# Hybrid decoder layer: last slots of four experts gathered and transposed as one tile, and 8 KB runs in the expert weight loads

## Chip, cores and metric

One core of one Trainium2 chip. The metric is the device time of one execution, in microseconds (us). The kernel before took 2277.39 us (median of 3 runs, 2274.5 to 2284.35).

## What is computed

A decoder layer on 2048 tokens of width 1024, all in float32. A mixer (gated linear attention and dilated attention) comes first; the change is in what follows it:

```
h = h + W_out [A ; B]
n = RMSNorm(h)
group  = argmax of 4 group logits;  two of its 8 experts by top-2   (32 experts in all)
h = h + sum over the two: gate * ( silu(n @ w1[e]) * (n @ w3[e]) ) @ w2[e]
y = RMSNorm(h)
```

w1 and w3 of an expert are 1024 x 512, w2 is 512 x 1024.

## The kernel before

The program is written in Tile: the code gives the data flow, and a scheduler that simulates the engines' time fixes the order of each engine's instructions when the program is built. On the chip every engine works through its list in order.

**Middle stage** (`mid`, lines 806 to 965, some 1183 to 1345 us). For each of 16 tiles of 128 tokens: output projection, residual, norm, router. VectorE writes the normed tile n2 in two halves of 512 columns (line 879); it is stored to HBM (line 880), and TensorE transposes it in blocks of 128 columns (line 891) against router weights loaded with row k*128 + p on partition p (lines 823, 824). `route` counts, for each expert, the slots that its tokens take, and scatters (token, gate) entries into a table in HBM. Each expert has 160 fixed slots: the first 128 are a full tile G, the last 32 a small tile R. Tokens beyond 160 would be done in a loop at the end, which does not run here.

**Expert stage** (`moe`, from line 1138). The loop at line 1371 runs over the 32 experts. In iteration e:
- `weights(e)` issues six loads of 1 MB on SyncE's queue (SP, line 1247): two halves each of w1, w3 and w2, into six buffers `raw`. A partition gets four rows of 2 KB that lie 128 rows apart (w1, w3), or two of 4 KB (w2). ScalarE (ACT) rounds each to `hi`, and VectorE (DVE) forms `lo` = raw - hi (line 1252).
- `gather(e + 2)` fetches, by indirect DMA on GpSimd (POOL), the 128 tokens of G (line 1263) and the 32 of R (line 1266).
- `up` multiplies the full tile in 48 matmuls (lines 1297 to 1299: hi by nh, hi by nl, lo by nh), and the 32 last slots by the unsplit weights in 32 matmuls (line 1306, two records each), four at a time in column groups: the remainder matmuls. They are the last readers of `raw`. Then h = silu * product (lines 1309, 1310; for the last slots 1314, 1315).
- `across` transposes h (line 1321) and the last slots' hr (line 1329) for the second product; ACT and DVE copy the results to hh, hl (line 1324) and ht (line 1331).
- `turn` transposes G of expert e + 1, eight blocks of 128 x 128 (line 1273), into tp, the only buffer of its pool in PSUM (2 of the 8 banks); ACT makes nh and DVE nl from it (line 1276). Then it transposes R, eight blocks of 32 x 128 (line 1281), and DVE copies it to nr (line 1283).
- `down` makes the second product: 24 matmuls for the full tile (lines 1343 to 1345), 16 remainder matmuls (line 1358, from ht), and adds both to HBM by indirect DMA (lines 1350, 1362).

For experts 0 and 1, G and a common R of 64 rows are gathered before the loop (lines 954 to 962). `entries` (line 1156) loads the table into SBUF: `it` for the full tiles, and `ir` four times, on each quarter of the partitions, for the last slots; these loads stand on SP's queue ahead of expert 1's weights.

Of the kernel before, what the change touches and what calls it, by code (L numbers as in the profile page):

```python
# [8 lines left out]
F32 = mybir.dt.float32  # L9
# [15 lines left out]
NE = 32  # L25
# [31 lines left out]
class Layer:  # L57
# [748 lines left out]
    def mid(self, st):  # L806
# [15 lines left out]
        nc.gpsimd.memset(rw, 0.0)  # L822
        nc.sync.dma_start(rw[:, :, 0:4], a["router_group_w"][0].rearrange("(k p) c -> p k c", p=128))
        nc.sync.dma_start(rw[:, :, 4:36], a["router_expert_w"][0].rearrange("(k p) c -> p k c", p=128))
        rb = keep.tile([128, NR], F32, name="rb")
# [32 lines left out]
        def project(i, between, oh, ol, h):  # L858
            rows = slice(i * 128, (i + 1) * 128)
            ss = wk.tile([128, 2], F32, name="ss")  # L860
            n2 = wk.tile([128, D], F32, name="n2")
            for f in range(2):
                pp = mm.tile([128, 512], F32, name="mm")
                fs = slice(f * 512, (f + 1) * 512)
                for k in range(4):
                    nc.tensor.matmul(pp, oh[:, k, :], woh[:, k, fs], start=k == 0, stop=False)
                    nc.tensor.matmul(pp, oh[:, k, :], wol[:, k, fs], start=False, stop=False)
                    nc.tensor.matmul(pp, ol[:, k, :], woh[:, k, fs], start=False, stop=k == 3)
                nc.vector.tensor_tensor(h[:, fs], pp, h[:, fs], OP.add)
                nc.scalar.activation(n2[:, fs], h[:, fs], AF.Square, accum_out=ss[:, f:f + 1])  # L870
                if f == 0:
                    between()
                    nc.vector.tensor_scalar(ss[:, 0:1], ss[:, 0:1], 1.0 / D, EPS, OP.mult, OP.add)
            nc.sync.dma_start(self.acc[rows, :], h)
            nc.vector.scalar_tensor_tensor(ss[:, 1:2], ss[:, 1:2], 1.0 / D, ss[:, 0:1], op0=OP.mult, op1=OP.add)
            nc.gpsimd.tensor_tensor(ss[:, 1:2], ss[:, 1:2], self.mhalf, OP.pow)
            for f in range(2):
                fs = slice(f * 512, (f + 1) * 512)
                nc.vector.scalar_tensor_tensor(n2[:, fs], h[:, fs], ss[:, 1:2], g2[:, fs], op0=OP.mult, op1=OP.mult)
            nc.sync.dma_start(self.n2[rows, :], n2)  # L880
            return n2
# [73 lines left out]
        R = self.e_in.tile([64, D], F32, name="R")  # L955
        self.first = {e: (G[e], R[32 * e:32 * e + 32], 32 * e) for e in range(2)}
        idx = rt.tile([128, 3], I32, name="idx", bufs=1)
# [180 lines left out]
    def moe(self):  # L1138
        tc, nc, a = self.tc, self.nc, self.a
        with self.moest as st:  # L1140
# [13 lines left out]
            i4A = keep.tile([128, NE], I32, name="i4")  # L1154

            def entries(es):

                ld = [nc.sync.dma_start(itA[:, es], table[0:128, es])]
                for g in range(4):
                    ld.append(nc.sync.dma_start(irA[32 * g:32 * g + 32, es], table[128:160, es]))  # L1160
                for l in ld:
                    for st in self.entries:
                        tc.add_manual_dep(l.ins, st.ins.name, mybir.DependencyInfo(mybir.DependencyClass.Sync, mybir.DependencyReason.DATA),
                                          reason="the whole table is read")
                f4 = gp.tile([128, NE], F32, name="f4", bufs=1)
                nc.vector.tensor_copy(f4[:, es], irA[:, es, 0])
                nc.vector.tensor_scalar(f4[:, es], f4[:, es], 4.0, self.gcol, OP.mult, OP.add)
                nc.vector.tensor_copy(i4A[:, es], f4[:, es])
# [66 lines left out]
            def weights(e, after={}):  # L1235

                parts = []
                for name, kk, n in (("expert_w1", 8, 512), ("expert_w3", 8, 512), ("expert_w2", 4, 1024)):
                    w = a[name][0, e] if isinstance(e, int) else a[name][0, bass.ds(e, 1)].rearrange("o k n -> (o k) n")
                    w = w.rearrange("(k p) n -> p k n", p=128)  # L1240
                    for half in range(2):
                        ks = slice(half * kk // 2, (half + 1) * kk // 2)
                        parts.append((w[:, ks, :], kk // 2, n))
                out = []
# [15 lines left out]
            def gather(e):  # L1260
# [3 lines left out]
                                             in_offset=bass.IndirectOffsetOnAxis(ap=itA[:, e, 0:1], axis=0))  # L1264
                R = gp.tile([32, D], F32, name="R")
                nc.gpsimd.indirect_dma_start(out=R, out_offset=None, in_=self.n2,
                                             in_offset=bass.IndirectOffsetOnAxis(ap=irA[0:32, e, 0:1], axis=0))
                return G, R

            def turn(G, R, at=0):  # L1270
                tp = tps.tile([128, KD, 128], F32, name="tp")
# [4 lines left out]
                self.turned = nc.scalar.copy(nh, tp), nc.vector.tensor_tensor(nl, tp, nh.bitcast(F32), OP.subtract)  # L1276
                if R is None:
                    return nh, nl, None
                tr = rps.tile([128, KD, 32], F32, name="r")
                for k in range(KD):  # L1280
                    nc.tensor.transpose(tr[:, k, :], R[:, k * 128:(k + 1) * 128], self.ident[at:at + 32, at:at + 32])
                nr = gp.tile([128, KD, 32], F32, name="nr")
                nc.vector.tensor_copy(nr, tr)  # L1283
                return nh, nl, nr

            def up(w, x):
                nh, nl, nr = x
                ps = []
# [19 lines left out]
                h = gp.tile([128, 512], F32, name="h")  # L1308
                nc.scalar.activation(h, ps[0], AF.Silu)
                nc.vector.tensor_tensor(h, ps[1], h, OP.mult)  # L1310
                hr = None
                if nr is not None:
                    hr = gp.tile([128, 256], F32, name="hr")
                    nc.scalar.activation(hr[64:128], pr[0:64], AF.Silu)
                    nc.vector.tensor_tensor(hr[64:128], pr[64:128], hr[64:128], OP.mult)
                return h, hr
# [47 lines left out]

            G = self.first
            x = turn(*G.pop(0))
            entries(slice(0, NE))
# [3 lines left out]
            for e in range(NE):  # L1371
                w1, w3, w2 = weights(e, held.get(e, lambda: {})())
                if e + 2 < NE:
                    G[e + 2] = gather(e + 2)
                h = across(*up((w1, w3), x))
                if e + 1 < NE:
                    x = turn(*G.pop(e + 1))
                    for t, c in zip(self.turned, self.crossed):
                        self.behind(t, c, "what the tensor engine waits for comes first")
# [13 lines left out]
            with tc.For_i(0, n, 1) as i:  # L1393
# [9 lines left out]
                w1, w3, w2 = weights(e)  # L1403
                x = turn(gx, None)
                down(w2, across(*up((w1, w3), x)), it, None)
# [96 lines left out]
```

## Time and profile before

| | |
|---|---|
| median of 3 runs | 2277.39 us |
| the profiled execution | 2277.6 us, of which the span is 2275.7 us |
| busy, share of the span | TensorE (PE) 92%, VectorE 56%, ScalarE 46%, GpSimd 22% |
| DMA | 440.32 MB, mean 193 GB/s over the span |
| loads of expert weights | 192, 1024 KB each, median 15.0 us from issue to landing |

The span runs from the first to the last instruction of the profiled execution. Idle time of an engine is put down to whatever released it last. A busy PE is not PE at its peak: matmuls overlap, so the time that one costs is read from the starts of successive ones. PEld is the weight load of TensorE, SP the queue that issues most transfers.

### The profile page before, as it was taken

The numbers are of one execution on the slowest core, as the hardware profiler recorded it, in microseconds if no ns is written. First come the engines' busy times: TensorE is split into PE (matmuls) and PEld (weight loads), VectorE is DVE, ScalarE is ACT, GpSimd is POOL, SyncE is SP. The second block draws the span as 40 slices with busy tenths as digits, with TensorE's granted clock in tenths as the row PEclk, the third lists the DMA queues.
The fourth block names the chain that finished last, engine by engine and source line by source line (L and its number), as shares of the span: only waits on it lengthen the run. The fifth ranks groups of instructions, "written<-read, shape, count | busy, mean of one in ns | idle before, by whom it ended". The sixth has DMA issues, their size and how long they took to land. (4 is left out here: it accounts for less than half of the span.)

```text
span 2275.7 us, 38854 instructions
## 1 busy us (share of the span) xinstructions
PE 2100.7 (92%) x15426; PEld 1566.0 (69%) x15426; DVE 1270.2 (56%) x2481; ACT 1056.1 (46%) x1805; POOL 509.6 (22%) x370
## 2 busy tenths in 40 slices
PE   7999999999996999999949967899999999999990
PEld 7799889799885665656637645566776677666660
DVE  5203436524336556666646564666777777677763
ACT  5413335523323466666714333555555555555552
POOL 2000000000002014152300241642233322233245
PEclk9999999999998999999979978999999999999995
DMA  8333333333318335444368737789988998888976
GB/s 257 116 113 93 108 128 103 124 100 111 107 66 275 103 98 142 126 136 98 85 167 296 250 80 215 230 291 298 306 288 277 301 299 303 291 275 293 302 254 233
DMA packets 248106, 440.32 MB, mean 193 GB/s; under 512 B 34497, under 2 KB 106594, under 8 KB 246626
## 3 DMA queue, kind: packets, MB, share of 16 engines
q1 hardware_dynamic: 198130, 351.39, 46.0%
q0 software_dynamic: 21840, 60.36, 10.5%
q10 hardware_dynamic: 27952, 26.05, 3.9%
q8 instruction: 123, 2.02, 0.4%
q14 instruction: 61, 0.50, 0.1%
HBM read 345.88 MB, written 92.40 MB: 193 GB/s over the span
## 5 line engine op out<-in xcount | busy, mean ns | idle before, releaser
L1252 DVE TENSOR_TENSOR lo<-raw,hi 128x2048 fp32r<-128x2048 f32 x192 | 439.2, 2290 | 163.7 <-ACT hi L1252 162.4
L1252 ACT CAST hi<-raw 128x2048 fp32r<-128x2048 f32 x192 | 365.6, 1906 | 253.7 <-DMA raw<-expert_w 218.8
L565 ACT ACTIVATE P<-P,st 128x256 f32<-128x256 f32 (+1 forms) x384 | 173.9, 455 | 112.7 <-DVE st L563 110.6
L214 PE MATMUL mm<-whi,nh 128*128 128x256 f32 x768 | 219.8, 286 | 0.0
L216 PE MATMUL mm<-whi,nl 128*128 128x256 f32 x768 | 218.0, 284 | 0.0
L215 PE MATMUL mm<-wlo,nh 128*128 128x256 f32 x768 | 217.6, 283 | 0.0
L1299 PE MATMUL mm<-lo,nh 128*128 128x512 f32 x512 | 203.7, 398 | 1.1 <-DVE lo L1252 1.1
L1297 PE MATMUL mm<-hi,nh 128*128 128x512 f32 x512 | 203.1, 397 | 1.0 <-ACT hi L1252 0.9
L1298 PE MATMUL mm<-hi,nl 128*128 128x512 f32 x512 | 200.4, 391 | 0.0
L129 POOL TENSOR_TENSOR ss<-ss,mhalf 128x1 f32<-128x1 f32 (+3 forms) x40 | 34.5, 864 | 696.3 <-DVE ss L128 694.8
L1350 POOL DMA_INDIRECT acc<-y,it x32 | 91.8, 2868 | 370.0 <-ACT y L1347 368.6
L563 DVE CUSTOM_DVE_ANT_0 P<-s,amask 128x256 f32<-128x256 f32 (+1 forms) x384 | 124.9, 362 | 75.3 <-PE s L559 58.8
L191 PE MATMUL mm<-nh,whi 128*128 128x512 f32 x384 | 154.5, 402 | 0.0
L1306 PE MATMUL r<-raw,nr 128*32 128x256 f32 x2048 | 152.7, 388 | 1.0 <-DVE nr L1283 0.5
L192 PE MATMUL mm<-nl,whi 128*128 128x512 f32 x384 | 153.1, 399 | 0.0
L193 PE MATMUL mm<-nh,wlo 128*128 128x512 f32 x384 | 152.7, 398 | 0.0
L214 PEld LDWEIGHTS mm<-whi,nh 128*128 128x128 f32 x768 | 145.2, 189 | 2.1 <-issue 0.7
L215 PEld LDWEIGHTS mm<-wlo,nh 128*128 128x128 f32 x768 | 145.5, 189 | 0.8 <-DVE wlo L177 0.4
L216 PEld LDWEIGHTS mm<-whi,nl 128*128 128x128 f32 x768 | 144.8, 189 | 0.1
L559 PE MATMUL s<-k,q 64*128 64x256 f32 (+1 forms) x768 | 137.5, 416 | 0.0
L1362 POOL DMA_INDIRECT acc<-yr,i x32 | 93.5, 2923 | 159.8 <-DMA acc<-y,it 148.8
L177 DVE TENSOR_TENSOR wlo<-raw,whi 128x1024 fp32r<-128x1024 f32 x48 | 57.0, 1221 | 112.7 <-ACT whi L176 112.7
(326 smaller groups left out, 4228.7 us busy)
## 6 DMA issues: line engine op xcount, KB each, us to landing
raw<-expert_w SPq DMA_DIRECT2D x192, 1024.0 KB, 15.0
raw<-w_in ACTq DMA_DIRECT2D x48, 512.0 KB, 4.9
fb<-fac SPq DMA_DIRECT2D x32, 384.0 KB, 7.6
x<-x SPq DMA_DIRECT2D x16, 512.0 KB, 5.2
og<-og SPq DMA_DIRECT2D x32, 256.0 KB, 3.3
xr<-x SPq DMA_DIRECT2D x32, 256.0 KB, 2.9
v<-av SPq DMA_DIRECT2D x8, 1024.0 KB, 6.1
hp<-xr SPq DMA_DIRECT2D x32, 256.0 KB, 2.5
```

The lines of the kernel that those rows point to most:

```text
L191: nc.tensor.matmul(ps, hi[:, k, ms], nh[q][:, k, :], start=k == 0, stop=False)
L192: nc.tensor.matmul(ps, hi[:, k, ms], nl[q][:, k, :], start=False, stop=False)
L193: nc.tensor.matmul(ps, lo[:, k, ms], nh[q][:, k, :], start=False, stop=k == KD - 1)
L214: nc.tensor.matmul(ps[:, j, :], h, hi[:, k, :], start=j == 0 and k == 0, stop=False, skip_group_check=True)
L215: nc.tensor.matmul(ps[:, j, :], h, lo[:, k, :], start=False, stop=False, skip_group_check=True)
L216: nc.tensor.matmul(ps[:, j, :], l, hi[:, k, :], start=False, stop=k == KD - 1, skip_group_check=True)
L565: nc.scalar.activation(P[:, h, 0:w], P[:, h, 0:w], AF.Exp, bias=nm, scale=-1.0, accum_out=dn)
L1252: split = nc.scalar.copy(hi, raw), nc.vector.tensor_tensor(lo, raw, hi.bitcast(F32), OP.subtract)
L1297: nc.tensor.matmul(ps[m], nh[:, k, :], hi[:, kk, :], start=k == 0, stop=False)
L1298: nc.tensor.matmul(ps[m], nl[:, k, :], hi[:, kk, :], start=False, stop=False)
L1299: nc.tensor.matmul(ps[m], nh[:, k, :], lo[:, kk, :], start=False, stop=k == KD - 1)
L1306: nc.tensor.matmul(pr[32 * g:32 * g + 32], nr[:, k, :], raw[:, k % 4, (g % 2) * 256:(g % 2) * 256 + 256], start=k == 0, stop=k == KD - 1, ...
```

## The change

The last 32 slots of four successive experts are gathered by one indirect DMA of 128 rows (64 for the last two experts), in iterations 0, 4, 8, ..., 28, and transposed as one tile of 128 columns in iterations 1, 5, ..., 29; each expert takes its 32 columns of the result. The token numbers for it come from a further table tile `irg`, loaded four more times. Weight rows are assigned to partitions so that a partition's rows lie next to each other (four rows of 2 KB, or two of 4 KB). To match, the columns of n2 and of h are written in another order: inside each half of n2 with steps of four columns, inside each half of h with steps of two.

```diff
-        nc.sync.dma_start(rw[:, :, 0:4], a["router_group_w"][0].rearrange("(k p) c -> p k c", p=128))
-        nc.sync.dma_start(rw[:, :, 4:36], a["router_expert_w"][0].rearrange("(k p) c -> p k c", p=128))
+        for f in range(2):
+            for n, c in (("router_group_w", slice(0, 4)), ("router_expert_w", slice(4, 36))):
+                nc.sync.dma_start(rw[:, 4 * f:4 * f + 4, c], a[n][0, f * 512:f * 512 + 512].rearrange("(p k) c -> p k c", k=4))
...
-                nc.vector.scalar_tensor_tensor(n2[:, fs], h[:, fs], ss[:, 1:2], g2[:, fs], op0=OP.mult, op1=OP.mult)
+                to = lambda t: t[:, fs].rearrange("t (p k) -> t k p", k=4)
+                nc.vector.scalar_tensor_tensor(n2[:, fs].rearrange("t (k p) -> t k p", k=4), to(h), ss[:, 1:2], to(g2), op0=OP.mult, op1=OP.mult)
...
+            irG = keep.tile([128, NE // 4, 2], I32, name="irg")
...
                     ld.append(nc.sync.dma_start(irA[32 * g:32 * g + 32, es], table[128:160, es]))
+                    n = (NE - 2 - g + 3) // 4
+                    ld.append(nc.sync.dma_start(irG[32 * g:32 * g + 32, 0:n], table[128:160, 2 + g:NE:4]))
...
-                    w = w.rearrange("(k p) n -> p k n", p=128)
+                    w = w.rearrange("(a p k) n -> a p k n", a=2, p=128)
...
-                R = gp.tile([32, D], F32, name="R")
-                nc.gpsimd.indirect_dma_start(out=R, out_offset=None, in_=self.n2,
-                                             in_offset=bass.IndirectOffsetOnAxis(ap=irA[0:32, e, 0:1], axis=0))
-                return G, R
-
-            def turn(G, R, at=0):
+                return G
+
+            def gather_last(g, n):
+                R = gp.tile([128, D], F32, name="R", bufs=1)
+                nc.gpsimd.indirect_dma_start(out=R[0:32 * n], out_offset=None, in_=self.n2,
+                                             in_offset=bass.IndirectOffsetOnAxis(ap=irG[0:32 * n, g, 0:1], axis=0))
+                return R
+
+            def turn(G):
...
-                tr = rps.tile([128, KD, 32], F32, name="r")
+                return nh, nl
+
+            def turn_last(R, n):
+                tp = tps.tile([128, KD, 128], F32, name="tp")
                 for k in range(KD):
-                    nc.tensor.transpose(tr[:, k, :], R[:, k * 128:(k + 1) * 128], self.ident[at:at + 32, at:at + 32])
-                nr = gp.tile([128, KD, 32], F32, name="nr")
-                nc.vector.tensor_copy(nr, tr)
-                return nh, nl, nr
+                    nc.tensor.transpose(tp[:, k, 0:n], R[0:n, k * 128:(k + 1) * 128], self.ident[0:n, 0:n])
+                nr = gp.tile([128, KD, 128], F32, name="nr", bufs=1)
+                nc.vector.tensor_copy(nr[:, :, 0:n], tp[:, :, 0:n])
+                return nr
...
-                nc.scalar.activation(h, ps[0], AF.Silu)
-                nc.vector.tensor_tensor(h, ps[1], h, OP.mult)
+                by, to = (lambda t: t.rearrange("t (a p k) -> t a k p", a=2, k=2)), (lambda t: t.rearrange("t (a k p) -> t a k p", a=2, k=2))
+                nc.scalar.activation(to(h), by(ps[0]), AF.Silu)
+                nc.vector.tensor_tensor(to(h), by(ps[1]), to(h), OP.mult)
...
-                    nc.scalar.activation(hr[64:128], pr[0:64], AF.Silu)
-                    nc.vector.tensor_tensor(hr[64:128], pr[64:128], hr[64:128], OP.mult)
+                    by, to = (lambda t: t.rearrange("t (p k) -> t k p", k=2)), hr[64:128].rearrange("t (k p) -> t k p", k=2)
+                    nc.scalar.activation(to, by(pr[0:64]), AF.Silu)
+                    nc.vector.tensor_tensor(to, by(pr[64:128]), to, OP.mult)
...
-            x = turn(*G.pop(0))
+            G, R = self.first
+            x = turn(G.pop(0))
+            nr, at = turn_last(R, 64), 0
             entries(slice(0, NE))
...
                 if e + 2 < NE:
                     G[e + 2] = gather(e + 2)
-                h = across(*up((w1, w3), x))
+                if e % 4 == 0 and e + 2 < NE:
+                    R = gather_last(e // 4, min(4, NE - 2 - e))
+                h = across(*up((w1, w3), x, nr[:, :, at:at + 32]))
+                at += 32
                 if e + 1 < NE:
-                    x = turn(*G.pop(e + 1))
+                    x = turn(G.pop(e + 1))
+                    if e % 4 == 1:
+                        nr, at = turn_last(R, 32 * min(4, NE - 1 - e)), 0
```

## Rows read from the trace of the kernel before

**Rows 1.** Busy time by stretch: us, PE, PEld, DVE, ACT, POOL, clock, DMA share, GB/s

```profile
1200.00:1330.00 130.00, 123.95 (x699) 95.69 (x697) 81.41 (x295) 49.28 (x119) 24.45 (x31) 0.96 0.77 257
1500.00:2200.00 700.00, 698.55 (x5116) 486.57 (x5115) 493.29 (x378) 389.69 (x302) 210.53 (x107) 1.00 0.89 293
```

**Rows 2.** Waits of PE, 1500 to 2200 us: total us, times, longest

```profile
PE mm L1297 <- ACT hi L1252: 0.9, 1, 0.9
```

**Rows 3.** Waits of SP's queue, 1400 to 2200 us

```profile
SPq L1247 <- PE r L1306: 492.0, 57, 17.6
```

**Rows 4.** Timeline of one iteration: start, duration, engine, line, count, idle before

```profile
1657.99 0.68 DVE L1310 TENSOR_TENSOR h<-mm,h 128x512 f32<-128x512 f32 x1
...
1658.69 1.09 PE L1273 MATMUL tp<-ident,G 128*128 128x128 f32 x8
...
1659.62 0.60 PE L1321 MATMUL mm<-ident,h 128*128 128x128 f32 x4
...
1660.15 0.33 PE L1329 MATMUL r<-ident,hr 64*128 64x64 f32 x2
...
1660.42 0.68 PE L1281 MATMUL r<-ident,R 32*128 32x32 f32 x8
1660.53 0.29 DVE L1331 COPY ht<-r 128x128 f32<-128x128 f32 x1 [0.83 <-PE r L1329]
...
1661.03 1.93 PE L1358 MATMUL r<-raw,ht 128*32 128x256 f32 x30
...
1662.20 1.22 DVE L1276 TENSOR_TENSOR nl<-tp,nh 128x1024 fp32r<-128x1024 f32 x1
...
1684.63 1.09 PE L1273 MATMUL tp<-ident,G 128*128 128x128 f32 x8
```

**Rows 5.** The transposes of R, all experts, from the costliest groups

```profile
L1281 PE MATMUL r<-ident,R 32*128 32x32 f32 x256 | 22.8, 230 | 4.2 <-DMA R<-n,idx 4.2
```

**Rows 6.** Timeline of PE in an earlier iteration with another order

```profile
1412.21 0.66 PE L1321 MATMUL mm<-ident,h 128*128 128x128 f32 x4
1412.70 1.04 PE L1273 MATMUL tp<-ident,G 128*128 128x128 f32 x8
...
1414.54 0.73 PE L1343 MATMUL mm<-hi,hh 128*128 128x512 f32 x2
```

**Rows 7.** Timeline: remainder matmuls between the main ones of `up`

```profile
1669.56 0.40 PE L1298 MATMUL mm<-hi,nl 128*128 128x512 f32 x1
...
1669.88 0.63 PE L1306 MATMUL r<-raw,nr 128*32 128x256 f32 x6
...
1670.45 0.50 PE L1297 MATMUL mm<-hi,nh 128*128 128x512 f32 x1
```

**Rows 8.** 1 MB loads: 2 KB runs (line 534), then 8 KB runs (line 536)

```profile
DMA to landing us min/median/max: 6.1/8.8/11.5
DMA to landing us min/median/max: 5.0/5.0/5.0
```

**Rows 9.** Timeline of the first two experts: table loads, weights, and their users

```profile
1360.56 5.61 SPq L1160 DMA_DIRECT2D ir<-table  x4
...
1367.31 55.39 SPq L1247 DMA_DIRECT2D raw<-expert_w  x12
...
1379.45 1.90 ACT L1252 CAST hi<-raw 128x2048 fp32r<-128x2048 f32 x1 [15.59 <-DMA raw<-expert_w]
...
1384.33 1.11 PE L1321 MATMUL mm<-ident,h 128*128 128x128 f32 x4 [11.38 <-DVE h L1310]
```

**Rows 10.** Plain and strided operands: ACT's reads from PSUM, then DVE

```profile
L201 ACT COPY o<-mm 128x512 f32<-128x512 f32 x32 | 18.5, 583 | 71.2 <-PE mm L193 69.4 <-issue 1.9
L199 ACT COPY o<-mm 128x512 f32<-128x512 f32 x16 | 9.3, 584 | 37.3 <-PE mm L193 36.1 <-issue 1.0
L631 DVE TENSOR_TENSOR f<-mn,nd x12: 273/364/377, 865.6 to 1150.8; 32x128 f32<-32x128 f32 x12
L879 DVE SCALAR_TENSOR_TENSOR n<-h,ss,g x32: 739/746/754, 1200.1 to 1322.0; 128x512 f32<-128x512 f32 x32
```

More of the change, by code (lines that the diff above doesn't have):

```diff
@@ L955, in mid @@
         R = self.e_in.tile([64, D], F32, name="R")
-        self.first = {e: (G[e], R[32 * e:32 * e + 32], 32 * e) for e in range(2)}
+        self.first = {0: G[0], 1: G[1]}, R
         idx = rt.tile([128, 3], I32, name="idx", bufs=1)
@@ L1239, in weights @@
                     w = a[name][0, e] if isinstance(e, int) else a[name][0, bass.ds(e, 1)].rearrange("o k n -> (o k) n")
-                    w = w.rearrange("(k p) n -> p k n", p=128)
+                    w = w.rearrange("(a p k) n -> a p k n", a=2, p=128)
                     for half in range(2):
-                        ks = slice(half * kk // 2, (half + 1) * kk // 2)
-                        parts.append((w[:, ks, :], kk // 2, n))
+                        parts.append((w[half], kk // 2, n))
                 out = []
@@ L1276, in turn, with up @@
                 self.turned = nc.scalar.copy(nh, tp), nc.vector.tensor_tensor(nl, tp, nh.bitcast(F32), OP.subtract)
-                if R is None:
-                    return nh, nl, None
-                tr = rps.tile([128, KD, 32], F32, name="r")
+                return nh, nl
+            def turn_last(R, n):
+                tp = tps.tile([128, KD, 128], F32, name="tp")
                 for k in range(KD):
-                    nc.tensor.transpose(tr[:, k, :], R[:, k * 128:(k + 1) * 128], self.ident[at:at + 32, at:at + 32])
-                nr = gp.tile([128, KD, 32], F32, name="nr")
-                nc.vector.tensor_copy(nr, tr)
-                return nh, nl, nr
-            def up(w, x):
-                nh, nl, nr = x
+                    nc.tensor.transpose(tp[:, k, 0:n], R[0:n, k * 128:(k + 1) * 128], self.ident[0:n, 0:n])
+                nr = gp.tile([128, KD, 128], F32, name="nr", bufs=1)
+                nc.vector.tensor_copy(nr[:, :, 0:n], tp[:, :, 0:n])
+                return nr
+            def up(w, x, nr=None):
+                nh, nl = x
                 ps = []
@@ L1363, in down @@
                                                        in_=yr, in_offset=None, compute_op=OP.add), e)
-            G = self.first
-            x = turn(*G.pop(0))
+            G, R = self.first
+            x = turn(G.pop(0))
+            nr, at = turn_last(R, 64), 0
             entries(slice(0, NE))
@@ L1403, in moe @@
                 w1, w3, w2 = weights(e)
-                x = turn(gx, None)
+                x = turn(gx)
                 down(w2, across(*up((w1, w3), x)), it, None)
```

## The prediction

> **What bounds the kernel now.** I first read the busy time by stretch, because the share over the whole span mixes stages. From 1500 to 2200 us, the bulk of the expert stage, PE is busy 698.55 of 700 us at a granted clock of 1.00, while DVE has 30% and POOL 70% to spare [rows 1]. Next come PE's waits there: the longest is a single one of 0.9 us, on a rounded weight [rows 2]. So the weights arrive in time. SP's queue itself stands 492.0 us waiting for the remainder matmuls to release a buffer [rows 3]: the loads follow PE, not the other way round. Last, the timeline: the transposes of G start at 1658.69 and, one expert later, at 1684.63, a period of 25.94 us filled end to end with PE work [rows 4]. The expert stage costs what PE's list costs. The first two experts are different: PE stands 11.38 us there, behind a weight that is late [rows 9]. The middle stage is also near PE's limit (123.95 of 130 us), with DVE at 81.41 [rows 1].
>
> **The transposes of R on PE.** They are removed in 31 loop iterations (256 records in blocks of eight are 32 blocks, one of them before the loop) [rows 5]. A block occupies PE from 1660.42 to the next start at 1661.03: 0.61 us [rows 4]. The upper end of the gain is 31 x 0.61 = 18.9 us. But this block is cover. After the transposes of hr at 1660.15, the next instruction is the remainder product, which reads ht. DVE writes ht from 1660.53 to 1660.82, while R is being transposed. Without R, PE stands until 1660.82 and a little more, say 1660.88 (an estimate: the 0.06 lies between the end of the transposes of hr, 1660.48, and DVE's start at 1660.53). The product then starts only 0.15 us earlier, so the lower end is 31 x 0.15 = 4.7 us [rows 4]. Whether the gap stays depends on the order that the scheduler chooses. An earlier iteration shows h transposed ahead of G (1412.21 against 1412.70) and the main product of `down` next; there the cover is not needed [rows 6]. Both orders occur, and nothing in the trace tells which one the new list takes. I take the middle, 0.38 us for an iteration: minus 11.8 us.
>
> **The joint transposes.** Eight blocks are added in the loop (iterations 1, 5, ..., 29). Eight transposes of 128 columns cost what G's cost, 1658.69 to 1659.62 = 0.93 us [rows 4]. They need tp, the only buffer of its pool, which is free once nl has been read from it, at 1662.20 + 1.22 = 1663.42. By then PE is in the main product of `down`, so the block probably sits between matmuls of another kind. What that costs is seen in `up`: from 1669.56 to 1670.45 are 0.89 us with six remainder records in between, against a matmul pace of 0.23 without them, so 0.66 us for the six and both changes of kind [rows 7]. Between 0 and 0.66 of this is the change of kind; half, 0.33, is the nearest I can get. A block then costs 0.93 to 1.26; I take 1.10. Eight of them: plus 8.8 us. The block before the loop replaces a smaller one and comes out even.
>
> **DVE, POOL and PSUM.** Four copies of nr become one of four times the columns; DVE has 30% free, and the remainder matmuls that read nr stand at the end of `up`: nothing. If that cover went, the copy would cost about nl's 1.22 us in eight iterations, 10 us. POOL issues one gather of R for every four experts instead of four, with 70% of its time free: nothing. It now waits for the `irg` loads, and behind it stand only gathers for experts two iterations ahead. R has one buffer now; its gather and its transposes are one iteration, 25.94 us, apart.
>
> **The weight loads.** Alone, 1 MB in 2 KB runs lands in 6.1 us at best, in 8 KB runs in 5.0 us [rows 8]. In the steady part the loads are hidden behind PE [rows 2, 3], so I cost the gain at nothing: what would become visible is only an earlier landing that PE does not wait for. In the start it counts. The four `ir` loads hold SP from 1360.56 for 5.61 us, and expert 1's weights come behind them at 1367.31 [rows 9]. Four `irg` loads with a quarter of the entries add about 5.61 / 4 = 1.4 us. The first weight lands 12.1 us after its issue, and PE's 11.38 us of idle time hang on it; the larger runs give back about 1.1 us. Sum: plus 0.3 us, with ends of minus 6 (the load lands as if alone) and plus 3 (SP's issue time is that of a full `ir` load for two of the four). The Trainium skill ("DMA: Bandwidth & Descriptors", Why small descriptors are slow) gives about three cycles of overhead to a packet, which for 2 KB against 8 KB is an estimate of only 3 to 4%; the row shows 18%. By that rule the loads would give back 0.2 us, and the sum would be 0.9 us higher.
>
> **Strided operands.** ACT reads PSUM with a step of four elements in 584 ns, plainly in 583 [rows 10]: silu with a step of two costs nothing more. For DVE, line 631 has both kinds: 273 ns plain, 364 to 377 with one strided operand, so about 0.7 to 0.8 ns for each element of 128 [rows 10]. For line 879 (two strided operands, 512 columns, 746 ns now) that bounds the extra at 0 to 0.8 us; with 32 of them, at most 26 us of DVE, in a stage where it has 48 us free [rows 1]. Only the last tile's is on the path to the router: I take plus 0.5 us, ends 0 and 1.6. For line 1310 (one strided operand in PSUM) it is up to 0.4 us. h is ready at 1658.67 and used at 1659.62, so it is hidden in the order of [rows 4], and not where h goes first. The router's two loads become four of the same entries, early in the stage: nothing.
>
> **The sum.** The profiled execution took 2277.6 us (span 2275.7), the median is 2277.39, so its durations can be used as they are. 2277.6 - 11.8 + 8.8 + 0.3 + 0.5 = 2275.4, rounded to 2275 us: no change that could be measured (0.5%, 11.4 us, is about what a measurement can tell). With the ends for the cover and the blocks alone it is 2267 to 2284.
>
> **Rival A: faster, because more was exposed than the steady part shows.** The order changes so that the whole 0.61 us is gained (minus 18.9 plus 8.8), and the start gains the 6 us of a load that lands as if alone: 2277.6 - 10.1 - 6 + 0.5 = 2262 us. For it: the order of [rows 6] exists, and PE's idle time of 11.38 us is one weight's. Against it: steady iterations, some two dozen, all have the other order.
>
> **Rival B: slower, a wait for tp in place of the transposes removed.** If the list puts the joint block right behind G, h and hr, as the code has it, PE stands at 1660.42 until nl is done at 1663.42: 3.0 us in eight iterations, with nothing behind it allowed to pass. 2277.6 - 4.7 + 8 x (0.93 + 3.0) + 0.8 = 2305 us. It decides as soon as the block stands more than half-way ahead of nl's end. Against it: the scheduler models tp's release, and elsewhere PE's list hardly waits [rows 2].
>
> **Rival C: slower, strided reads on DVE.** If h's transposes go first in all iterations and line 1310 takes 0.4 us more, PE waits for it 31 times: plus 12.4; with 1.6 in the middle stage and the forecast's other terms, 2275.4 + 12.4 + 1.1 = 2289 us. The Trainium skill ("SBUF — State Buffer", Specifications) says that SBUF has lines of 16 bytes and that each step to a new line costs; line 879's new step of four elements is exactly one line. By that rule it takes the full 0.8 us; line 631, whose step is larger, agrees with it.
>
> **That the change doesn't do what it says** would be seen in the loads alone (same landing times), and the forecast holds without them.
>
> **Chances.** Forecast 0.55, A 0.22, B 0.13, C 0.10. A counts as faster, B as slower, C half as slower; each edge of the forecast adds a little: faster 0.24, same 0.57, slower 0.19. The likeliest case alone spans 2266 to 2285. The range reaches to A and its bound on one side and past C on the other, and leaves out most of B: 2257 to 2294.
>
> **What would show it.** Right: a period of 25.94 less 0.15 to 0.61 us in three iterations of four and about 0.5 to 1.1 more in the fourth; line 1281's transposes gone and nine blocks of the joint ones; PE waiting for ht in the order of [rows 4]. Loads that land sooner without any effect on the period. Wrong: PE waiting for nl or for raw weights in `down`; a period that falls by a microsecond or more, which would mean that the loads did bound; line 879 doubled with PE waiting for n2 in the middle stage; a change of more than 6 us before the third expert.

## The result, and the profile after

The changed kernel takes 2258.25 us (median of 8 runs, 2254.14 to 2265.57) against 2275.94 us for the kernel before (8 runs): ratio 0.9923, 95% interval 0.9909 to 0.9937. That is 0.8% faster, more than the 0.5% that a measurement can tell, and it is the case of rival A in direction and nearly in size (2262), not the forecast of no change. It lies inside the stated range (2257 to 2294), 1.25 us above the lower end. The profiled execution took 2256.75 us (span 2255.0).

Where the 20.7 us between the two spans went is seen when both are cut at the same events: near the first n2, and at the first transposes of G, the first up matmul of the sixth expert, that of the last expert, and the last matmul of `down`. The view is the busy time by stretch; its second number is the length of the stretch. The kernel before:

```profile
1183.80:1346.80 163.00, 140.06 (x766) 108.00 (x767) 106.24 (x379) 60.70 (x132) 37.64 (x43) 0.90 0.70 226
1346.80:1513.50 166.70, 143.76 (x974) 98.01 (x975) 92.27 (x93) 67.09 (x53) 71.76 (x46) 0.88 0.71 217
1513.50:2190.70 677.20, 675.75 (x4941) 470.93 (x4940) 477.93 (x364) 377.32 (x291) 202.08 (x102) 1.00 0.89 294
2190.70:2218.70 28.00, 24.71 (x171) 16.64 (x169) 17.61 (x14) 12.44 (x13) 18.15 (x11) 1.00 0.67 214
```

The kernel after, the same view (its first and third stretch answer to those of [rows 1]):

```profile
1183.80:1347.50 163.70, 140.10 (x766) 107.84 (x766) 118.83 (x382) 59.42 (x132) 37.70 (x43) 0.91 0.70 225
1347.50:1505.50 158.00, 139.41 (x943) 97.11 (x944) 92.39 (x87) 68.76 (x53) 62.81 (x42) 0.92 0.71 233
1505.50:2170.60 665.10, 664.31 (x4785) 465.38 (x4783) 473.18 (x345) 379.92 (x290) 158.59 (x84) 1.00 0.84 297
2170.60:2195.80 25.20, 23.06 (x150) 15.78 (x148) 17.35 (x14) 11.30 (x11) 14.46 (x9) 1.00 0.65 217
```

The last numbers of a line are the granted clock, the DMA share and GB/s. The reader is to see two gains, 8.7 us in the first five experts and 12.1 in the steady part, and that PE is still full in the steady part (664.31 of 665.10 us). PE did not get faster; its list got shorter. The last expert (minus 2.8) and the end behind it (57.0 us before, 59.2 after) nearly cancel, and the middle stage is as long as it was, though DVE works 12.6 us more there.

**The steady part.** The timeline of one iteration shows what the list became. It answers to [rows 4], and its order is that of [rows 6]: h is transposed ahead of G. (L1335 transposes h, L1283 G, L1343 hr; L1345 writes ht, L1372 is the remainder product that reads it.)

```profile
1598.34 0.66 PE L1335 MATMUL mm<-ident,h 128*128 128x128 f32 x4
1598.83 1.04 PE L1283 MATMUL tp<-ident,G 128*128 128x128 f32 x8
...
1599.80 0.33 PE L1343 MATMUL r<-ident,hr 64*128 64x64 f32 x2
...
1600.06 0.73 PE L1357 MATMUL mm<-hi,hh 128*128 128x512 f32 x2
...
1600.26 0.28 DVE L1345 COPY ht<-r 128x128 f32<-128x128 f32 x1
...
1605.84 1.93 PE L1372 MATMUL r<-raw,ht 128*32 128x256 f32 x32
...
1624.04 0.49 PE L1283 MATMUL tp<-ident,G 128*128 128x128 f32 x3
...
1631.04 0.63 PE L1372 MATMUL r<-raw,ht 128*32 128x256 f32 x6
1631.61 1.09 PE L1292 MATMUL tp<-ident,R 128*128 128x128 f32 x8
1632.63 1.91 PE L1372 MATMUL r<-raw,ht 128*32 128x256 f32 x26
...
1650.47 0.60 PE L1283 MATMUL tp<-ident,G 128*128 128x128 f32 x4
```

The product that reads ht now comes at 1605.84, 5.3 us after ht is written: the main product of `down` stands between them and is the new cover. G to G is 25.21 us in an ordinary iteration (25.20 to 25.33 but for one of 25.84; three ordinary ones and one joint one make 102.2 us, where four iterations before made 103.76), so all 0.61 us of the block of R came off, and about 0.09 more, whose cause is not shown. In a joint iteration G to G is 1650.47 - 1624.04 = 26.43 us, 1.19 more than the 25.24 in the middle of the others: the block itself, 1631.61 to 1632.63, takes 1.02, and the rest is the break in the remainder matmuls.

PE's waits from 1500 to 2190 stay as good as none ([rows 2]: one of 0.9; now five under 0.8 each). In the waits of SP's queue, the row that answers to [rows 3] still names PE's remainder matmuls (total, times, longest):

```profile
SPq L1253 <- PE r L1317: 434.2, 56, 18.9
```

The weights land sooner, 10.4 us after the issue instead of 15.0 (median of 192), and PE is as full as before.

**The start.** The timeline of PE after the first transposes, before:

```profile
1352.93 1.05 PE L1281 MATMUL r<-ident,R 32*128 32x32 f32 x8 [4.16 <-DMA R<-n,idx]
1354.50 3.64 PE L1306 MATMUL r<-raw,nr 128*32 128x256 f32 x32 [0.52 <-DVE nr L1283]
1358.07 0.75 PE L1297 MATMUL mm<-hi,nh 128*128 128x512 f32 x2
...
1381.38 2.29 DVE L1252 TENSOR_TENSOR lo<-raw,hi 128x2048 fp32r<-128x2048 f32 x1 [8.22 <-ACT hi L1252]
```

and after, with the rows that answer to [rows 9] (ACT's silu, SP's loads of expert 1's weights, DVE's index work, the first transposes of h):

```profile
1350.57 1.22 PE L1308 MATMUL mm<-hi,nh 128*128 128x512 f32 x2 [1.10 <-ACT nh L1286]
...
1364.45 0.60 ACT L1322 ACTIVATE h<-mm 128x512 f32<-128x512 f32 x1 [3.56 <-PE mm L1310]
...
1372.98 1.90 SPq L1253 DMA_DIRECT2D raw<-expert_w  x4
...
1377.22 0.18 DVE L1173 CAST f<-ir 128x32 f32<-128x32 int32 x1 [18.24 <-DMA ir<-table]
1377.32 2.29 DVE L1258 TENSOR_TENSOR lo<-raw,hi 128x2048 fp32r<-128x2048 f32 x1
...
1379.90 0.69 DVE L1323 TENSOR_TENSOR h<-mm,h 128x512 f32<-128x512 f32 x1
...
1380.64 1.12 PE L1335 MATMUL mm<-ident,h 128*128 128x128 f32 x4 [9.92 <-DVE h L1323]
```

Before, PE waited 4.16 us for the gather of R and did 32 remainder records ahead of the first up matmul; after, the up matmuls begin 7.5 us earlier, and all 64 remainder records come behind them. What holds h changes, too. Before, ACT and DVE had expert 1's first weight ahead of it in their lists: `hi` waited 15.59 us for the load [rows 9], DVE's `lo` 8.22 us for `hi`, and h came behind. After, silu is done early (1364.45), but PE still stands 9.92 us for h, because DVE, at the head of its list, stands 18.24 us for the index table (L1173) with a `lo` behind it. So half of the 7.5 us is given back before the first transposes of h, which come 3.7 us earlier than before (1380.64 against 1384.33 in [rows 9]). The granted clock of the stretch is 0.92 instead of 0.88; how much of the 8.7 us that makes up is not separated.

### The profile page after: what moved, and what is told of

Its sections match the earlier page's. It is cut to its first block, busy times and chain, and to the rows that moved or that the text cites. A ratio compares the mean times of both kernels' runs of the same rounds, so it can differ in the third digit from the quotient of the medians.

```text
span 2255.0 us, 38488 instructions
## 1 busy us (share of the span) xinstructions
PE 2085.3 (92%) x15242; PEld 1559.9 (69%) x15242; DVE 1278.5 (57%) x2458; ACT 1059.5 (47%) x1805; POOL 455.9 (20%) x348
## 5 line engine op out<-in xcount | busy, mean ns | idle before, releaser
L214 PEld LDWEIGHTS mm<-whi,nh 128*128 128x128 f32 x768 | 145.7, 190 | 2.0 <-issue 0.7
L1317 PE MATMUL r<-raw,nr 128*32 128x256 f32 x2048 | 142.9, 383 | 0.0
L1310 PEld LDWEIGHTS mm<-lo,nh 128*128 128x128 f32 x512 | 96.6, 189 | 42.9 <-issue 21.0
## 6 DMA issues: line engine op xcount, KB each, us to landing
raw<-expert_w SPq DMA_DIRECT2D x192, 1024.0 KB, 10.4
```

Source lines behind the costliest of these rows:

```text
L214: nc.tensor.matmul(ps[:, j, :], h, hi[:, k, :], start=j == 0 and k == 0, stop=False, skip_group_check=True)
L1310: nc.tensor.matmul(ps[m], nh[:, k, :], lo[:, kk, :], start=False, stop=k == KD - 1)
L1317: nc.tensor.matmul(pr[32 * g:32 * g + 32], nr[:, k, :], raw[:, k % 4, (g % 2) * 256:(g % 2) * 256 + 256], start=k == 0, stop=k == KD - 1, ...
```

## The experiments

The two halves of the change come first, each alone.

**The joint tile alone**: the changed kernel with the loads and columns of the kernel before.

```diff
-                    w = w.rearrange("(a p k) n -> a p k n", a=2, p=128)
+                    w = w.rearrange("(k p) n -> p k n", p=128)
...
-                nc.scalar.activation(to(h), by(ps[0]), AF.Silu)
+                nc.scalar.activation(h, ps[0], AF.Silu)
```

> The joint gather and transposes alone; weights in 2 KB runs and columns in the old order, as before. Theory (TensorE's list sets the expert stage, the loads are hidden): the same period as in the changed kernel, 25.2 us in ordinary iterations and 26.4 us in those with the joint block, and a total of 2255 to 2261 us (ratio to before 0.991 to 0.994). Rival (the 8 KB runs are what made it faster): a total of 2268 to 2278 us, with TensorE waiting for rounded weights.

2263.3 us (6 runs) beside 2281.09 for the kernel before on the same chip: 0.9918 (0.9903 to 0.9933), as much as the whole change (0.9923). The order of PE's list is the new one. In its timeline, the transposes of G at the start of a joint iteration and of the next:

```profile
1627.26 1.04 PE L1281 MATMUL tp<-ident,G 128*128 128x128 f32 x8
...
1653.69 1.04 PE L1281 MATMUL tp<-ident,G 128*128 128x128 f32 x8
```

26.43 us, as in the changed kernel; the shortest ordinary ones are 25.21 to 25.26. Its profiled execution, one of its slower ones, has some iterations that are 0.4 to 1.5 us longer, with PE waiting for hr (6.4 us at nine times from 1500 to 2200); the changed kernel waits for it once, 0.6 us. The absolute time lay a little above what was expected, where the kernel before was slower too.

**The longer runs alone**: the kernel before with the new loads and columns.

```diff
-                    w = w.rearrange("(k p) n -> p k n", p=128)
+                    w = w.rearrange("(a p k) n -> a p k n", a=2, p=128)
...
-                nc.vector.scalar_tensor_tensor(n2[:, fs], h[:, fs], ss[:, 1:2], g2[:, fs], op0=OP.mult, op1=OP.mult)
+                to = lambda t: t[:, fs].rearrange("t (p k) -> t k p", k=4)
+                nc.vector.scalar_tensor_tensor(n2[:, fs].rearrange("t (k p) -> t k p", k=4), to(h), ss[:, 1:2], to(g2), op0=OP.mult, op1=OP.mult)
```

> The 8 KB runs and the column orders alone; R gathered and transposed for each expert. Theory: period 25.94 us as before, the loads land sooner (about 10 us in place of 15) and nothing follows from it: 2274 to 2279 us (ratio 0.999 to 1.002). Rival (the runs gain): 2262 to 2269 us.

2278.76 us (12 runs) against 2281.09: 0.9986 (0.9977 to 0.9996), some 2 us, 1 to 5 by the interval. PE's list has the old order, and in the timeline G to G is what it was to the last digit:

```profile
1606.97 1.09 PE L1275 MATMUL tp<-ident,G 128*128 128x128 f32 x8
...
1632.91 1.09 PE L1275 MATMUL tp<-ident,G 128*128 128x128 f32 x8
```

25.94 us. The loads did become cheaper for the DMA engines. From 1600 to 2100 us the queue that carries them (packets, MB, share of 16 engines) goes from the first line, of the kernel before, to the second, of this one:

```profile
q1 hardware_dynamic: 50490, 119.62, 66.3%
```

```profile
q1 hardware_dynamic: 16416, 119.54, 61.2%
```

A third of the packets, the same bytes, and 8% less of the engines' time (66.3% to 61.2%); the two loads of [rows 8] differ by 18% in time to landing. From the about three cycles of overhead to a packet in the Trainium skill ("DMA: Bandwidth & Descriptors", Why small descriptors are slow) follows an estimate of 3 to 4% for 2 KB against 8 KB. The trace has more, 8%. None of it is on the path in this order of the list, where the period stays the same. So the gain of the steady part comes with the joint tile, and the runs alone give 1 to 5 us elsewhere. This version also has the strided reads of n2, which have a price of their own (see below), so the 2 us are the sum of both.

**Is it the order?** The theory says that the old block of R was cover for ht, and that the gain is whole only because the new list puts h ahead of G. Two experiments turn the order alone. First, the changed kernel with G's transposes held ahead of h's:

```diff
-                    nc.tensor.transpose(tp[:, k, :], h[:, k * 128:(k + 1) * 128], self.ident)
+                    t = nc.tensor.transpose(tp[:, k, :], h[:, k * 128:(k + 1) * 128], self.ident)
+                    if after is not None:
+                        self.behind(t, after, "the next tile's transposes come first")
```

> The changed kernel, with G's transposes ordered ahead of h's from iteration 5 on, as they stood in the kernel before. Theory (R's transposes were cover for the copy ht; the gain hangs on the order): TensorE stands about 0.45 us before the remainder product, period 25.7 to 25.8 us in ordinary iterations, and a total 11 to 14 us above the changed kernel, 2268 to 2273 us. Rival (the removed transposes are saved in any order): 2256 to 2260 us, period 25.2 to 25.35 us.

2287.32 us, 1.0024 (1.0010 to 1.0037) of the kernel before: the gain is gone. Its timeline, to be laid beside [rows 4]:

```profile
1597.35 1.09 PE L1286 MATMUL tp<-ident,G 128*128 128x128 f32 x8
...
1598.28 0.60 PE L1341 MATMUL mm<-ident,h 128*128 128x128 f32 x4
...
1598.91 0.59 ACT L1346 CAST hh<-mm 128x512 fp32r<-128x512 f32 x1 [1.03 <-PE mm L1341]
1599.18 0.29 DVE L1353 COPY ht<-r 128x128 f32<-128x128 f32 x1 [0.83 <-PE r L1351]
...
1599.57 1.93 PE L1380 MATMUL r<-raw,ht 128*32 128x256 f32 x30 [0.43 <-ACT hh L1346]
...
1623.21 1.09 PE L1286 MATMUL tp<-ident,G 128*128 128x128 f32 x8
```

Where the transposes of R stood, PE stands 0.43 us, until ht (done at 1599.47) and hh (1599.50) are there. The iteration is 25.85 to 25.88 us: of 0.61 us only 0.09 is gained. The total is higher than expected by the joint blocks, which still cost their 1.2 us, and perhaps by the start, whose fourth iteration took 44.6 us in the profiled execution.

Second, the kernel before, with its R, but h ahead of G:

```diff
-                    nc.tensor.transpose(tp[:, k, :], G[:, k * 128:(k + 1) * 128], self.ident)
+                    t = nc.tensor.transpose(tp[:, k, :], G[:, k * 128:(k + 1) * 128], self.ident)
+                    if after is not None:
+                        self.behind(t, after, "this expert's transposes come first")
```

> The kernel before, with h's transposes ordered ahead of G's from iteration 4 on, as they stand in the changed kernel; R's transposes stay. Theory (nothing idles in either order while R is there): period 25.85 to 25.94 us, 2272 to 2277 us. Rival (the other order alone makes the gain): period 25.2 to 25.4 us, 2260 to 2266 us.

2288.94 us, 1.0027 (1.0015 to 1.0039): a miss. The order by itself gains nothing; the block of R is still paid, and in the timeline something else is late:

```profile
1586.03 1.90 ACT L1252 CAST hi<-raw 128x2048 fp32r<-128x2048 f32 x1 [1.69 <-DMA raw<-expert_w]
1587.96 2.29 DVE L1252 TENSOR_TENSOR lo<-raw,hi 128x2048 fp32r<-128x2048 f32 x1 [1.19 <-ACT hi L1252]
1588.46 0.66 PE L1323 MATMUL mm<-ident,h 128*128 128x128 f32 x4
1588.95 1.04 PE L1273 MATMUL tp<-ident,G 128*128 128x128 f32 x8
...
1590.77 0.34 PE L1331 MATMUL r<-ident,hr 64*128 64x64 f32 x2 [0.79 <-DVE hr L1317]
1591.04 0.68 PE L1283 MATMUL r<-ident,R 32*128 32x32 f32 x8
```

DVE still had a `lo` to finish (until 1590.25) ahead of hr, and PE waited for hr at 17 iterations, 8.7 us together. So neither half does it: it takes the order and the missing block.

The `lo` is late because `hi` waited for its load. With h first and runs of 2 KB, PE waits for hr in both versions (this one, and the joint tile alone); in the nine profiles with h first and runs of 8 KB these waits come to 0.8 us at most. So where h goes first, PE feels the loads, and the longer runs take that wait away. In the medians it does not show: the joint tile alone is as fast as the whole change. But it also lacks the strided reads of n2, and the two may cancel. Plain n2 with runs of 8 KB (below) came to 0.9884 and then 0.9918 of the kernel before, the joint tile alone, also with plain n2, to 0.9918: that leaves 0 to 8 us for the runs.

**The price of a bad place for the joint block** (rival B): seven joint blocks held right behind the transposes of hr, ahead of `down`.

```diff
+            def mul(*args, **k):
+                i = nc.tensor.matmul(*args, **k)
+                if self.first_is:
+                    self.behind(i, self.block, "the joint block comes first")
+                return i
...
-                        nc.tensor.matmul(py, hh[:, k, :], hi[:, k % 2, fs], start=k == 0, stop=False)
+                        mul(py, hh[:, k, :], hi[:, k % 2, fs], start=k == 0, stop=False)
```

> The changed kernel with the joint block of seven iterations ordered right behind the transposes of hr, ahead of the down matmuls, where it must wait for its gather or for the turned tile's buffer. Rival B's price, 3.0 us at each of them, would make the total about 21 us longer (2275 to 2282 us where the changed kernel has 2258), joint iterations 29.4 us instead of 26.4. If nothing is late there, joint iterations stay at 26.4 us and the total within 3 us of the changed kernel's.

2265.66 us, 0.9966 (0.9953 to 0.998), where the changed kernel on the same chip ran 2259.65 us, 0.9937 (0.9923 to 0.995). The timeline of a joint iteration has the wait, and for the reason named, nl's end at 1631.88:

```profile
1630.65 1.23 DVE L1286 TENSOR_TENSOR nl<-tp,nh 128x1024 fp32r<-128x1024 f32 x1 [0.41 <-ACT nh L1286]
...
1631.98 1.07 PE L1292 MATMUL tp<-ident,R 128*128 128x128 f32 x8 [2.14 <-issue]
```

But it is 2.14 us, not 3.0, since nl too comes earlier when h goes first; and the joint iteration grows only by 0.67, to 27.10 us, in five of the seven (by 2.1 in the first and 2.4 in the last). The rest is made good in the same iteration: the remainder matmuls of `up` come as one run of 64 records in 3.59 us, where the ordinary iteration has them in three pieces of 10, 8 and 46 that take 4.27 us and break the up matmuls. Both theories' numbers were missed: a real wait, at a fifth of the price that rival B had for it in those five, and 6.0 us in the total.

**DVE's wait in the start.** The changed kernel with the places' three small instructions put behind iteration 0's transposes:

```diff
-                nc.vector.tensor_copy(f4[:, es], irA[:, es, 0])
+                self.behind(nc.vector.tensor_copy(f4[:, es], irA[:, es, 0]), after, "what the tensor engine waits for comes first")
...
+                if e == 0:
+                    places_of(slice(0, NE), self.turned[1])
```

> The changed kernel with VectorE's work for the places of the last slots put behind iteration 0's turn, so that VectorE does not stand at the index table while TensorE waits for h. Theory (VectorE's wait for the table holds up the first transposes of h): TensorE's idle time of 9.9 us ahead of them falls by 4 to 9 us and the total is as much below the changed kernel, 0.996 to 0.998 of it. Rival (the weights' arrival sets that moment, or the first joint gather becomes late instead): the total stays within 2 us.

2250.68 us, 0.9897 (0.9882 to 0.9912) of the kernel before, 9 us below the changed kernel on the same chip. The timelines of the two starts; the changed kernel there (first transposes of G at 1354.86):

```profile
1385.42 1.12 PE L1335 MATMUL mm<-ident,h 128*128 128x128 f32 x4 [6.61 <-DVE h L1323]
```

and this one (first transposes of G at 1348.48):

```profile
1371.21 0.66 PE L1337 MATMUL mm<-ident,h 128*128 128x128 f32 x4
...
1380.53 0.18 DVE L1175 CAST f<-ir 128x32 f32<-128x32 int32 x1 [5.47 <-DMA ir<-table]
```

From G's to h's transposes it is 22.7 us instead of 30.6: 7.8 less, so the theory holds for this wait, and PE's wait for h is gone. But the rival's reason, the weights' arrival, holds for what comes next, where PE now stands for expert 1's first weight:

```profile
1385.10 0.80 PE L1310 MATMUL mm<-hi,nh 128*128 128x512 f32 x1 [4.55 <-ACT hi L1260]
```

The next iteration, from G to G, takes 32.5 us instead of 27.0, and at the transposes of the sixth expert's G only 2.3 of the 7.8 us are left. Where the 9 us come from is so only in part known: the two profiled executions differ by 10.7 us, 2.3 of it in the start and 2.7 in the steady part, where the ordinary iteration is 25.12 us instead of 25.24 (why was not followed). Some 6 lie ahead of the first transposes of G, and 3.9 of these ahead of the first n2, where no difference is expected. The changed kernel of this comparison stood as expected:

> The changed kernel once more, for comparison on the same chip. Both theories: 0.992 of the kernel before (0.990 to 0.994), iterations of 25.2 us, joint ones 26.4, the first up matmul of expert 5 some 158 us after expert 0's first transposes.

**The strided reads.** The changed kernel with n2 and the router's weights in plain order. The experts' weights stay in the new order of rows, so this version leaves out the match of columns and rows, and its experts compute other numbers:

```diff
-                nc.vector.scalar_tensor_tensor(n2[:, fs].rearrange("t (k p) -> t k p", k=4), to(h), ss[:, 1:2], to(g2), op0=OP.mult, op1=OP.mult)
+                nc.vector.scalar_tensor_tensor(n2[:, fs], h[:, fs], ss[:, 1:2], g2[:, fs], op0=OP.mult, op1=OP.mult)
```

> The changed kernel with the normalised tokens written in plain column order and the router's weights as before, so that VectorE reads nothing at a stride in SBUF; the experts then multiply token columns with other rows of their weights (the routing stays what it was). Theory: the strided reads cost 0.41 us on each of the 32 instructions and lie beside other work, so n2 goes back to 0.75 us, the middle stage loses 13 us of VectorE's busy time, and the total is 0 to 1.5 us below the changed kernel. Rival (strided reads on the path): 5 to 13 us below it.

The reads cost what was said. The durations of the changed kernel's line 882, in ns (lowest, median, highest), which answer to the last of [rows 10]:

```profile
L882 DVE SCALAR_TENSOR_TENSOR n<-h,ss,g x32: 1123/1156/1201, 1200.0 to 1322.3; 128x512 f32<-128x512 f32 x32
```

In plain order they are back at 748. The total, though, was 2248.96 us (4 runs), 0.9884 (0.9869 to 0.9899), 10.7 us below the changed kernel: the rival's number. Since no stage of the profile showed such a saving, it was taken again, with the changed kernel beside it, and with a version that moves the stride to PE's reads of the gathered tiles (the joint tile's too), which computes what the changed kernel does:

> The changed kernel a third time, to stand beside the next three on one chip. Both theories: 0.993 of the kernel before (0.991 to 0.995).

> The kernel plain_n2 once more (normalised tokens in plain column order, the experts multiplying other rows of their weights), which came out 10.7 us below the changed kernel where 0 to 1.5 had been expected. If VectorE's strided reads do cost the total some 10 us, it is again 8 to 12 us below the changed kernel of this call. If the first result was chance in the length of the stages ahead of the experts, whose profile shows no such saving, it is 0 to 4 us below.

```diff
-                    nc.tensor.transpose(tp[:, k, :], G[:, k * 128:(k + 1) * 128], self.ident)
+                    nc.tensor.transpose(tp[:, k, :], G[:, k // 4 * 512 + k % 4:k // 4 * 512 + 512:4], self.ident)
```

> The changed kernel with the stride moved from VectorE's 32 reads of the normalised tokens to TensorE's transposes of the gathered tiles, which read every fourth column (router weights as before, weight runs still of 8 KB). If TensorE reads such columns as fast as neighbours, its total is that of plain_n2_again within 2 us, the eight transposes of a gathered tile still 0.97 us, an iteration 25.2 us. If it pays for the stride, the eight take 1.2 us or more and an iteration 25.5 us or more, and the total is 5 us or more above plain_n2_again.

The changed kernel took 2267.65 us there (0.9933, 0.9917 to 0.9948), plain n2 2262.76 (0.9918, 0.9904 to 0.9933), the stride on PE 2269.26 (0.9945, 0.9928 to 0.9962). So the second time plain n2 was 4.9 us below, between the two expectations. On PE the stride costs 0.09 us in each tile, 1.06 us from the first of the eight transposes to the next work instead of 0.97 (timeline):

```profile
1609.46 1.13 PE L1280 MATMUL tp<-ident,G 128*128 128x128 f32 x8
1610.52 0.34 PE L1340 MATMUL r<-ident,hr 64*128 64x64 f32 x2
```

and the iteration 25.33 instead of 25.24, 2.8 us over 31. What plain n2 gains stays open: 10.7 us in one comparison, 4.9 in the other, and only about 1 if the 2.8 is taken off the version with the stride on PE. From the first n2 to the first transposes of G the seven profiles with plain n2 take 145.7 to 151.0 us (mean 147.9), the seven with strided n2 147.5 to 155.4 (mean 150.5): some 2.6 us in the mean, with ranges that overlap. Elsewhere, too, single executions differ by as much. In the third profile of the changed kernel the timeline has a stretch in the fourth iteration in which PE, ACT and DVE all stand, for no cause that the profile names ("remote" and "issue"):

```profile
1450.69 0.38 ACT L1328 ACTIVATE hr<-r 64x256 f32<-64x256 f32 x1 [11.33 <-remote]
...
1451.59 0.47 PE L1343 MATMUL r<-ident,hr 64*128 64x64 f32 x2 [5.98 <-issue]
```

The fourth and fifth iterations together took 64.6 us there, 58.6 and 58.8 in the first two profiles, 58.0 and 61.1 with plain n2. All four profiles of this last comparison have the stretch (ACT stands 9.6 to 13.6 us ahead of that hr), and the first two of the changed kernel do not, so its times are to be held only against those of the same comparison.

**Both together**: the stride on PE, and the places late.

> pe_stride and late_places together, the version that should be fastest: if both gains stand beside each other, 9 us below pe_stride of this call, 0.984 to 0.988 of the kernel before. If they are one and the same gain (the start of the experts getting free of VectorE), no more than 4 us below the better of the two, about 0.988.

2262.42 us, 0.991 (0.9894 to 0.9926): 6.8 us below the stride on PE alone, 5.2 below the changed kernel beside it. It falls between the two expectations, and its ratio is not better than that of the late places alone (0.9897), which is the lowest of the versions that leave the computation as it is (0.9882 to 0.9912, against 0.9894 to 0.9926 here: the two are not told apart).

## Where the prediction was right and where it was wrong

The measured 2258.25 us lies in the stated range, but at its edge, and it is there because the range was drawn to reach rival A (chance 0.22). The likeliest case, no change at 2275 us with a span of 2266 to 2285, did not come. In the steady part the mechanism was right: PE's list sets the time, the block of R was cover for ht, and the order decides what its removal gains. What failed is a size there, and the account of the start.

**The step that failed** is the one at the transposes of R: "nothing in the trace tells which one the new list takes. I take the middle, 0.38 us". The two orders were named rightly, and both ends measured: 0.09 us of gain with G first (predicted 0.15), 0.70 with h first (predicted 0.61). But the middle of two orders is not something that a list can take: every ordinary iteration of the steady part took h first. The forecast should have been one of two times. By its own other terms, with 0.61 for all 31, it would have been 2268; with 0.15, 2283. The second has a run beside it: G first came out 6 us above the kernel before, and 2283 is 5 above the 2277.6 that the sum starts from. With the measured 0.70 and 1.19, 31 x 0.70 = 21.7 less 8 x 1.19 = 9.5 is a net 12.2 us, where the forecast had 3.0.

Why h went first can't be settled by these runs, only that it goes with the joint tile: the longer runs alone kept the old order, the joint tile alone took the new one.

**The start** was sized at plus 0.3 us from table loads and weights, with an end of minus 6. In the profiled executions it gained 8.7. The first load did land nearly as if alone, 6.4 us after its issue in the longer runs alone (1375.72 to 1382.12) where it was 12.1 before; but the loads are not what moved h in the changed kernel, where expert 1's weights are issued later (1372.98 against 1367.31 in [rows 9]). What changed is the lists: PE's first up matmuls no longer stand behind the gather of R and 32 remainder records, and h no longer behind expert 1's first weight. The prediction read the 11.38 us rightly as that weight's, but took for granted that the new lists would keep h behind it. In the changed kernel h waits for the table's index instead, and with that wait moved the weight is what PE waits for next. How the 8.7 us divides is argued from single timelines, not shown. Executions of one kernel differ there by 12 us (158.0, 156.0 and 168.0 us in the three profiles of the changed kernel), so 8.7 is a size of two single executions, not of the medians: the medians' 17.7 us less the 12.1 of the steady part and about 0.6 of the end leave some 5 for the start and the middle stage.

**The joint block**, 1.10 us, was right in place and nearly in size: 1.02 for the block, 1.19 with the break in the remainder matmuls. It sits between matmuls of another kind, as was said.

**Loads costed at nothing** in the steady part: right for the old order, where a third of the packets left the period at 25.94 us. In the order that came it was not quite nothing: without the longer runs PE waits for hr, 6.4 us in the profile of the joint tile alone.

**Strided operands.** 0.41 us for line 879's successor lies in the range of 0 to 0.8, about 0.8 ns for each element of a partition. The Trainium skill ("SBUF — State Buffer", Specifications) has a penalty for each step to a new line. The trace agrees that there is one, at half of the 0.8 us that the prediction worked out from rows for the full case and put down to that rule. On the path 0.5 us was taken; the runs leave some 1 to 11 open, so this term was probably too small, and the DVE time that was called free in the middle stage perhaps not wholly so. Rival C's other half didn't come: h went first, but the reads from PSUM with a step of two cost next to nothing, on ACT (598 ns against 600) or on DVE (691 against 683).

**The rivals.** A came out by its first half (the order) as it was priced. Its 6 us in the start came in size by another way than A had it, so that 2262 lies so near to 2258 is in part luck. B's mechanism is real, but the list avoids it; forced, it waits 2.1 us and costs 0.67 in most joint iterations, not 3.0, because the iteration's other work closes up behind the wait.

**Its signs.** The period fell by 0.70 us, a little more than the 0.15 to 0.61 that were to show it right, and PE waited 0.43 us for ht and hh where G was held first. None of its signs of being wrong was seen: nothing in the steady part, and 4.4 us before the third expert's transposes (1412.70 against 1408.27) where more than 6 would have counted.

## What to carry to other kernels

Before removing an instruction from a full engine, look at what is produced while it runs: the removal is worth its length only if something else can stand there, and the order of the list, which a scheduler may choose anew, decides that. Where two orders are possible, forecast two times with chances, not the mean; building the same edit with the order forced either way separates what the removal is worth from what the order is worth. And in a start where everything is late, follow the waits past the first that goes away: moving an index computation took 7.8 us off one wait, and the next weight took 5.5 of them back.

## What the hardware showed that was not expected

A DVE instruction that reads two SBUF operands with a step of four floats takes 1156 ns for 512 columns instead of 747, while reads from PSUM with a step of two floats took 691 instead of 683 on DVE and 598 instead of 600 on ACT. PE's transposes of columns four apart cost 0.09 us in eight. Remainder matmuls in one run of 64 records took 3.59 us, in three pieces 4.27. A wait of 2.1 us on a full PE lengthened its iteration by only 0.67 in five cases of seven. With h transposed first and weight runs of 2 KB, PE waited 6.4 and 8.7 us for hr, behind a late load; with runs of 8 KB at most 0.8, though the loads looked hidden in the old order.
